# HGRN's first scaled level reads its keys from the forget gate, and the unit's output is written into the gate's own tile

## The chip, the cores and the metric

The kernel runs on one core of a Trainium2 chip. The metric is the device time of one launch in microseconds (us), smaller is better. Engine names are those of the profile: PE is TensorE's matmuls, PEld its weight loads, DVE is VectorE, ACT is ScalarE, POOL is GpSimd, SP is SyncE, which here only issues DMAs.

## The reference

The layer takes x (2048 rows of 1024, float32) through a mixer and a feed-forward part. The mixer has two groups of heads side by side; HGRN2 is the one that the change touches.

```python
def _hgrn2_mixer(q_raw, f_raw, i_raw, g_raw, lb, norm_w):
    f = lb + (1.0 - lb) * jax.nn.sigmoid(f_raw.astype(f32))
    q = heads(jax.nn.silu(q_raw.astype(f32))) * (HG_HEAD_DIM ** -0.5)
    k = heads(1.0 - f)
    logf = heads(jnp.log(f))
    v = heads(i_raw.astype(f32))
    o = _hgrn2_chunk_scan(q, k, v, logf)
    o = o * lax.rsqrt(jnp.mean(o * o, axis=-1, keepdims=True) + NORM_EPS)
    o = o.reshape(B, T, HG_WIDTH) * norm_w.astype(f32) * jax.nn.silu(g_raw.astype(f32))
...
def reference(...):
    proj = h @ w_in[l]
    ...
    x = x + jnp.concatenate([o_hg, o_rw], axis=-1) @ w_out[l]
    x = x + _conv_ffn(_rmsnorm(x, norm2_w[l]), w_up[l], conv_w[l], conv_b[l], w_down[l])
```

The scan is `o_t = S_t^T q_t` with `S_t = diag(f_t) S_{t-1} + k_t v_t^T`, per head of 128 columns. The keys are one minus the forget gate. The other group is RWKV-7, whose state update also has a solve of small triangular systems.

## The kernel before

Time is cut into 4 blocks of 512 steps. In the first part of the program (to about 1320 us) three streams are recorded in turn, a piece of each at a time: the *dense* stream (input projections, tile names pj, hh, hl, wh, wl, and output projections of finished blocks), the *RWKV* stream (`rw_super`, eight pieces, each two pairs of heads of one block) and the *HGRN* stream (`hg_unit`, sixteen units, one head of one block each, numbered here 0 to 15). All matmuls of the projections are three fp32r products (lines 270 to 272). The second part of the program, the feed-forward, comes after.

A scheduler takes the recorded instructions and sets a fixed order on each engine; an engine then runs its own list in that order and waits by semaphores for the others. Buffers come from pools: a tag names a ring of buffers, and a new tile of that tag waits until the readers of the tile that held the buffer have ended, a DMA that reads it included.

An HGRN unit takes q, f, v and the output gate gg from the projections (tags hq, hf, hv, hgg, two buffers each). Line 947 makes the keys k on VectorE in the one buffer of tag hk. Then come seven levels of `scaled`: at each, line 965 makes the query half of a tile X (tag hX, three buffers) by VectorE, and the key half is made by line 971, or at level 0 by a ScalarE copy; the running product Pf, which is f's own tile, and the running factor Sf are updated by lines 974 and 972. All ScalarE activations pass through the helper at line 122, so their line says 122 and the tile names tell them apart. The levels' matmuls are line 990 (and 997, 1046), masked into A and copied to Af. The state runs through lines 1044 to 1059, the output product through 1064 and 1065. The norm is the tail of the unit: squares into a tile osq that takes over the hk buffer, split into two parts, lines 1083 and 1084 sum them, and lines 1076 and 1077 multiply by the norm and the gate. Line 1078 stores the result to the DRAM tile oT, on SP's queue or, in the last block, on POOL's. Line 370 writes the gate tile when the projection's sum is evicted.

In the RWKV stream the names that matter are, in the order of the work: TZ and TTs, the inverted triangular blocks (lines 808, 814, and matmuls 821 and 834), L847, which applies them, the ScalarE copies of its results to UV and M, L867, the first matmul that needs the PSUM buffer which those copies free, and L881, whose results L884 and L887 (M and AR) take up on VectorE. L905 is the step of its state recurrence. Line 313 is the token shift of a projection's result rkv, and lines 241 to 243 are sums of tiles for the feed-forward, loaded from h2d.

Of the kernel before, what the change touches and what calls it, by code (L numbers as in the profile page):

```python
# [11 lines left out]
AF = mybir.ActivationFunctionType  # L12
# [6 lines left out]
P = 128  # L19
# [48 lines left out]
def tile_layer(ctx, tc, consts, x, norm1_w, w_in, hg_lb_logits, hg_norm_w, rw_shift_mu, rw_w0, rw_w2,  # L68
# [4 lines left out]
    V, S, TE = nc.vector, nc.scalar, nc.tensor  # L73
# [40 lines left out]
    def act(out_, in_, func, **kw):  # L114

        want = tables.get(func)
        if want is not None and want != tab["now"]:
            pre = S.preload_act_table_set(want)
            for u_ in tab["uses"]:
                tc.add_manual_dep(pre.ins, u_.ins.name, NOSYNC, reason="table order")  # L120
            tab.update(now=want, pre=pre, uses=[])
        i_ = S.activation(out_, in_, func, **kw)  # L122
        if want is not None:
            tc.add_manual_dep(i_.ins, tab["pre"].ins.name, NOSYNC, reason="table order")
            tab["uses"].append(i_)
        return i_
# [57 lines left out]
    oT = [dp.tile([D, BLK], F32, name=f"oT{b}") for b in range(NBLK)]  # L184
# [89 lines left out]
    def phase1(c1):  # L274
# [353 lines left out]
        def last_dma(nb):  # L628

            return nc.gpsimd.dma_start if nb == NBLK - 1 else dma  # L630
# [313 lines left out]
        def hg_unit(nb, j):  # L944
            q, f, v, gg = (stage.pop((n_, nb, j)) for n_ in "qfvg")
            k = rp.tile([P, BLK], F32, tag="hk", name="hk")
# [13 lines left out]
            def scaled(l):  # L960

                m = 1 << l
                X = rp.tile([P, BLK], F32, tag="hX", name="hX", bufs=3)
                vw = lambda t_: t_.rearrange("p (n e m) -> p n e m", e=2, m=m)
                V.tensor_mul(vw(X)[:, :, 1, :], vw(q)[:, :, 1, :], vw(Pf)[:, :, 1, :])
                n_ = BLK // (2 * m)
                if l == 0:
                    act(vw(X)[:, :, 0, :], vw(k)[:, :, 0, :], AF.Copy)
                    act(vw(Sf)[:, :, 0, :], vw(Pf)[:, :, 1, :], AF.Copy)
                else:  # L970
                    V.tensor_mul(vw(X)[:, :, 0, :], vw(k)[:, :, 0, :], vw(Sf)[:, :, 0, :])
                    V.tensor_mul(vw(Sf)[:, :, 0, :], vw(Sf)[:, :, 0, :],
                                 vw(Pf)[:, :, 1, m - 1:m].broadcast_to([P, n_, m]))
                V.tensor_mul(vw(Pf)[:, :, 1, :], vw(Pf)[:, :, 1, :],
                             vw(Pf)[:, :, 0, m - 1:m].broadcast_to([P, n_, m]))
                return X
# [32 lines left out]
            for l in range(3):  # L1009
                Xs.append(scaled(l))  # L1010
                yield
# [9 lines left out]
            for l in range(3, 6):  # L1021
                Xs.append(scaled(l))
                yield
# [9 lines left out]
            for c0 in range(0, P, 32):  # L1033
                act(Af[c0:c0 + 32, :, c0:c0 + 32], A[c0:c0 + 32], AF.Copy)
            yield
            X = scaled(6)
            V.tensor_mul(k, k, Sf)
            V.tensor_mul(q, q, Pf)
# [27 lines left out]
            sq = rp.tile([P, BLK], F32, tag="hk", name="osq")  # L1066
# [7 lines left out]
            act(sq, sq, AF.Exp, scale=-0.5)  # L1074
            yield
            V.tensor_mul(sq, op, sq)
            V.tensor_mul(sq, sq, gg)
            last_dma(nb)(oT[nb][j * P:(j + 1) * P, :], sq)
            done["hg"] += 1
            yield  # L1080

# [10 lines left out]
        def hg_stream():  # L1092
            for n in range(4 * NBLK):
                while ready["hg"] <= n:
                    yield None
                yield from hg_unit(n // 4, n % 4)
# [528 lines left out]
```

## Time and profile before

| | |
|---|---|
| median of 3 runs | 2646.72 us (2646.23 to 2655.82) |
| the profiled execution | 2645.42 us, span 2643.6 us |
| granted TensorE clock, mean | 0.994 |
| PE busy | 2547.0 us, 96% of the span |
| DVE busy | 1963.7 us, 74% |
| ACT busy | 1372.7 us, 52% |
| POOL busy | 382.1 us, 14% |
| HBM traffic | 192 GB/s over the span |
| chain that ended last | PE 70%, DVE 11%, ACT 8%, DMA 7%, issue 3% |

The profile is one execution. A row of a group gives line, engine, operation, output and inputs, shapes and count, then the busy time and the mean time of one, then the idle time of the engine before them and what ended it. A row of the timeline gives start and duration in us. In a row of waits the waiting instruction stands on the left of the arrow and the one that released it on the right.

### The profile page before, as it was taken

To read this page: it belongs to the slowest core of one execution; us is meant where nothing else is said; L and a number is where in the kernel's file an instruction comes from. 1 tells how busy PE (TensorE), PEld (TensorE's weight loads), DVE (VectorE), ACT (ScalarE), POOL (GpSimd) and SP (SyncE) were. 2 spreads that over 40 slices of the span, in tenths; PEclk is the share of its full clock that TensorE was granted. 3 is DMA by queue.
4 is the path that set the end of the run, shared out by engine and by line. 5 is a ranking of instruction groups with operands and counts; after the bars stand their busy time and mean duration, and the time that the engine had idled before them with its cause. 6 is when DMAs were issued, how large, how long until landed. Compare 5 with 4: busy or idle time off the path is not lost.

```text
span 2643.6 us, 51054 instructions
## 1 busy us (share of the span) xinstructions
PE 2547.0 (96%) x19467; PEld 2046.8 (77%) x19467; DVE 1963.7 (74%) x3744; ACT 1372.7 (52%) x2258; POOL 382.1 (14%) x686
## 2 busy tenths in 40 slices
PE   7999999999999999899899999999999999999998
PEld 5877777777777767777678888887888887888887
DVE  4868677676576765777678789988988887766556
ACT  5555444555545555344466654556554544545444
POOL 6433222212222122232100000000000000000000
PEclk9999999999999999999999999999999999999999
DMA  8846463555655565845583467747763553998655
GB/s 304 239 147 195 152 168 116 143 159 205 190 173 138 174 212 179 261 151 150 181 287 124 136 221 257 240 154 232 245 203 129 171 171 128 334 321 283 200 191 187
DMA packets 380298, 518.98 MB, mean 196 GB/s; under 512 B 114463, under 2 KB 211093, under 8 KB 380053
## 3 DMA queue, kind: packets, MB, share of 16 engines
q1 hardware_dynamic: 325521, 337.38, 40.1%
q0 software_dynamic: 54464, 178.32, 20.9%
q8 instruction: 153, 2.51, 0.4%
q14 instruction: 92, 0.75, 0.1%
q10 hardware_dynamic: 68, 0.02, 0.0%
HBM read 372.99 MB, written 134.22 MB: 192 GB/s over the span
## 4 chain that ended last, share of the span: by engine, by line
PE 70%; DVE 11%; ACT 8%; DMA 7%; issue 3%; POOL 0%; SPq 0%; DVEq 0%; ACTq 0%; POOLq 0%
PE pj L270 7%; PE pj L271 7%; PE pj L272 6%; PE ua L270 5%; PE ua L272 5%; PE ua L271 5%; PE da L271 3%; PE da L272 3%; PE da L270 3%; PE ud L271 2%; PE ud L270 2%; PE ud L272 2%; PE db L272 2%; PE db L271 2%; PE db L270 2%
## 5 line engine op out<-in xcount | busy, mean ns | idle before, releaser
L270 PE MATMUL pj<-hh,wh 128*128 128x512 f32 x960 | 391.6, 408 | 6.1 <-ACT rkv L122 4.0
L271 PE MATMUL pj<-hl,wh 128*128 128x512 f32 x960 | 377.4, 393 | 0.0
L272 PE MATMUL pj<-hh,wl 128*128 128x512 f32 x960 | 377.4, 393 | 0.0
L270 PE MATMUL ua<-Bh,uwh 128*128 128x512 f32 x704 | 276.4, 393 | 3.5 <-ACT m L122 2.2
L272 PE MATMUL ua<-Bh,uwl 128*128 128x512 f32 x704 | 274.3, 390 | 0.0
L271 PE MATMUL ua<-Bl,uwh 128*128 128x512 f32 x704 | 274.1, 389 | 0.0
L270 PEld LDWEIGHTS pj<-hh,wh 128*128 128x128 f32 x960 | 180.9, 189 | 54.5 <-issue 7.0
L272 PEld LDWEIGHTS pj<-hh,wl 128*128 128x128 f32 x960 | 180.8, 188 | 39.4 <-DMA wl<-Win171l 0.3
L271 PEld LDWEIGHTS pj<-hl,wh 128*128 128x128 f32 x960 | 181.0, 189 | 35.0 <-DVE hl L488 0.5
L254 ACT CAST uwh<-uraw 128x512 fp32r<-128x512 f32 x220 | 134.3, 617 | 135.0 <-PE ua L271 55.7
L255 DVE TENSOR_TENSOR dal<-draw,dah 128x512 fp32r<-128x512 f32 x138 | 95.2, 690 | 108.3 <-ACT dah L254 105.7
L255 DVE TENSOR_TENSOR uwl<-uraw,uwh 128x512 fp32r<-128x512 f32 x220 | 147.1, 684 | 34.3 <-ACT uwh L254 34.3
L254 ACT CAST dah<-draw 128x512 fp32r<-128x512 f32 x138 | 85.8, 621 | 160.0 <-PE da L271 75.5
L270 PEld LDWEIGHTS ua<-Bh,uwh 128*128 128x128 f32 x704 | 132.2, 188 | 33.9 <-ACT m L122 5.6
L272 PEld LDWEIGHTS ua<-Bh,uwl 128*128 128x128 f32 x704 | 132.2, 188 | 28.1 <-DVE uwl L255 0.4
L271 PEld LDWEIGHTS ua<-Bl,uwh 128*128 128x128 f32 x704 | 132.3, 188 | 26.7
L270 PE MATMUL ud<-Bh,uwh 128*128 128x512 f32 x352 | 138.0, 392 | 0.0
L1495 POOL DMA_DIRECT2D gd<-y x2 | 1.1, 542 | 943.1 <-DVE y L1493 943.1
L272 PE MATMUL ud<-Bh,uwl 128*128 128x512 f32 x352 | 137.1, 390 | 0.0
L271 PE MATMUL ud<-Bl,uwh 128*128 128x512 f32 x352 | 137.0, 389 | 0.0
L271 PE MATMUL da<-dbl,dah 128*128 128x512 f32 x332 | 129.4, 390 | 0.2 <-DVE dbl L255 0.2
L272 PE MATMUL da<-dbh,dal 128*128 128x512 f32 x332 | 129.2, 389 | 0.0
(582 smaller groups left out, 6203.0 us busy)
## 6 DMA issues: line engine op xcount, KB each, us to landing
uraw<-in_w_up_dram SPq DMA_DIRECT2D x176, 256.0 KB, 3.2
woraw<-in_w_out_dram POOLq DMA_DIRECT2D x96, 256.0 KB, 3.6
br<-gd SPq DMA_DIRECT2D x88, 256.0 KB, 4.3
draw<-Sg SPq DMA_DIRECT2D x88, 256.0 KB, 3.0
draw<-Tw SPq DMA_DIRECT2D x88, 256.0 KB, 3.9
gd<-y SPq DMA_DIRECT2D x86, 256.0 KB, 3.0
Sg<-br SPq DMA_DIRECT2D x72, 256.0 KB, 2.2
xt<-x1d SPq DMA_DIRECT2D x32, 512.0 KB, 6.5
```

The lines of the kernel that those rows point to most:

```text
L254: S.copy(hi, src)
L255: V.tensor_sub(lo, src, hi.bitcast(F32))
L270: TE.matmul(acc, lh, rh, start=first, stop=False, skip_group_check=skip)
L271: TE.matmul(acc, lh, rl, start=False, stop=False, skip_group_check=skip)
L272: TE.matmul(acc, ll, rh, start=False, stop=last, skip_group_check=skip)
L1495: (dma if end is None else nc.gpsimd.dma_start)(gd_[2 * h + b][fb * P:(fb + 1) * P, :], ys[0][:, b * BLK:(b + 1) * BLK])
```

## The change

At level 0 the key half of X is now computed by ScalarE from the even columns of f as −1·f + 1, where it was a copy of k's even columns. The tile k itself is still made on VectorE, for the diagonal matmuls, the later levels and the state. And the last product of the unit is written into the gate's tile gg, from which the store then reads; the squares' tile in the hk buffer is then free once VectorE has read it.

```diff
                 if l == 0:
-                    act(vw(X)[:, :, 0, :], vw(k)[:, :, 0, :], AF.Copy)
+                    act(vw(X)[:, :, 0, :], vw(f)[:, :, 0, :], AF.Identity, bias=1.0, scale=-1.0)
                     act(vw(Sf)[:, :, 0, :], vw(Pf)[:, :, 1, :], AF.Copy)
...
             V.tensor_mul(sq, op, sq)
-            V.tensor_mul(sq, sq, gg)
-            last_dma(nb)(oT[nb][j * P:(j + 1) * P, :], sq)
+            V.tensor_mul(gg, sq, gg)
+            last_dma(nb)(oT[nb][j * P:(j + 1) * P, :], gg)
```

The number of instructions per engine stays; the scheduler's order moves. Three places matter below. On ScalarE, at the start of unit 1, the copy stood between the token shift's rkv with a weight cast and the copies of UV and M:

```order
 L122 ACTIVATE rkv_1763<-pj,omu 128x512
 L254 CAST wh<-wraw 128x512
-L122 ACTIVATE hX<-hk 128x256
 L122 ACTIVATE UV<-rw 64x4x128 x4
 L122 ACTIVATE M<-rw 128x8x64
```

It is gone from there. Unit 1's copy now stands some thirty instructions earlier on ScalarE, between the eviction of its v (hv) and a cast, ahead of unit 0's copies to Af. The other odd units changed alike.

On VectorE, at the start of unit 13, just behind the last product of unit 12:

```order
-L1077 TENSOR_TENSOR osq<-osq,hgg 128x512
-L241 TENSOR_TENSOR xt<-xt 128x1024
-L242 TENSOR_TENSOR xt<-xt 128x1024
+L1077 TENSOR_TENSOR hgg<-osq,hgg 128x512
 L947 TENSOR_SCALAR hk<-hf 128x512
-L313 SCALAR_TENSOR_TENSOR rkv_13175<-pj,vt,rkv_13175 128x511
-L314 SCALAR_TENSOR_TENSOR rkv_13175<-lastc,vt,rkv_13175 128x1
 L974 TENSOR_TENSOR hf<-hf 128x256
-L315 COPY lastc<-pj 128x1
 L971 TENSOR_TENSOR hX<-hk,Sf 128x128x2
 L965 TENSOR_TENSOR hX<-hq,hf 128x128x2
 L972 TENSOR_TENSOR Sf<-Sf,hf 128x128x2
```

The keys and the first level's products moved ahead of the two sums of tiles (L241, L242) and of the token shift. Those come behind, then three products of the next level among them, and then L884 and L887.

On TensorE, between units 10 and 11, in the RWKV solve:

```order
+L834 MATMUL rw<-TTs,ZT 32x32
 L1083 MATMUL hg<-part,ones 128x512
-L270 MATMUL pj<-wh,hh 128x512
-L271 MATMUL pj<-wl,hh 128x512
-L270 MATMUL pj<-wh,hh 128x512
-L271 MATMUL pj<-wl,hh 128x512
+L834 MATMUL rw<-TTs,ZT 32x32 x31
+L1084 MATMUL hg<-part,ones 128x512
+L847 MATMUL rw<-RHS,TTs 64x128 x2
 L272 MATMUL pj<-wh,hl 128x512 x2
```

The solve's L821, L834 and L847 now come earlier among the projection matmuls, with the sums of unit 10's norm (L1083, L1084) in their midst, and L847 follows L834 directly where ten projection matmuls stood between them.

## The prediction

> **What bounds the kernel now.** I read the page's sums first, then busy time by stretch, then who waited for whom, then the timeline around the named waits.
>
> ```profile
> PE 2547.0 (96%) x19467; PEld 2046.8 (77%) x19467; DVE 1963.7 (74%) x3744; ACT 1372.7 (52%) x2258; POOL 382.1 (14%) x686
> ...
> core 0: us, PE busy (x) PEld busy (x) DVE busy (x) ACT busy (x) POOL busy (x), PEclk, DMA share, GB/s
> 60.00:1320.00 1260.00, 1194.66 (x13501) 935.24 (x13499) 882.50 (x2088) 637.02 (x1063) 329.47 (x592) 0.99 0.58 176
> 1320.00:2643.60 1323.60, 1307.92 (x5776) 1076.10 (x5776) 1052.51 (x1590) 705.14 (x1138) 14.04 (x26) 1.00 0.64 211
> ```
>
> TensorE is busy 96% of the span at a granted clock of 0.99 or 1.00. The change lies in the stretch from 60 to 1320 us, where the sixteen HGRN units run between the projections. There TensorE is idle 1260 − 1194.7 = 65.3 us. The change removes no matmul, so its gain is cut out of these 65.3 us (2.5% of the span). The question is which of that idle time ends on the two edited lines.
>
> ```profile
> PE rw L867 <- ACT M L122: 9.7, 6, 3.6
> PE rw L881 <- DVE AR L887: 4.3, 1, 4.3
> ...
> ACT hX L122 <- DVE hk L947: 20.1, 10, 5.8
> DVE M L884 <- PE rw L881: 16.8, 10, 5.3
> ...
>   DMA oT<-osq: 3.0, 2
> ```
>
> The columns are total us, times, longest. The second longest wait of TensorE is an RWKV matmul, L867, that waits for ScalarE's copy of M; it is no HGRN instruction. ScalarE in turn stands 20.1 us in ten waits for the HGRN keys, L947. The last row is VectorE's idle time before L947: twice it waited for the output store of the unit before. The timeline of unit 1 joins them (start, duration, engine, instruction; the idle time before it and its releaser in brackets):
>
> ```profile
> 143.68 0.69 DVE L1077 TENSOR_TENSOR osq<-osq,hgg 128x512 f32<-128x512 f32 x1
> 144.23 2.32 PE L847 MATMUL rw<-RHS,TTs 64*64 64x128 f32 x62
> 145.15 0.61 ACT L254 CAST wh<-wraw 128x512 fp32r<-128x512 f32 x1
> 148.94 0.43 DVE L947 TENSOR_SCALAR hk<-hf 128x512 f32<-128x512 f32 x1 [2.11 <-DMA oT<-osq]
> 149.40 0.45 ACT L122 ACTIVATE hX<-hk 128x256 f32<-128x256 f32 x1 [3.65 <-DVE hk L947]
> 149.86 2.40 ACT L122 ACTIVATE UV<-rw 64x512 f32<-64x512 f32 x4
> 152.27 1.82 ACT L122 ACTIVATE M<-rw 128x512 f32<-128x512 f32 x3
> 152.92 2.35 PE L867 MATMUL rw<-UV,KBT 128*64 128x64 f32 x37 [3.56 <-ACT M L122]
> ```
>
> Unit 0's output sits in the keys' buffer until its store has landed; then L947 writes the keys, ScalarE copies them, and only behind that copy, in ScalarE's order, come UV and M. So TensorE pays 3.56 us for a key copy of 0.45 us.
>
> **The change part by part.** *The copy from the gate.* It no longer reads k, and leaves its place ahead of UV (the ScalarE rows above). UV can then start when its matmul L847 has ended or ScalarE is free, whichever is later. In unit 1 that is 144.23 + 2.32 = 146.55 instead of 149.86: 3.31 us earlier, all of it inside the stall of 3.56, so 3.31 gained. Three other odd units show the same pattern:
>
> ```profile
> 292.85 2.13 PE L847 MATMUL rw<-RHS,TTs 64*64 64x128 f32 x62
> 296.39 2.41 ACT L122 ACTIVATE UV<-rw 64x512 f32<-64x512 f32 x4
> 299.46 1.26 PE L867 MATMUL rw<-UV,KBT 128*64 128x64 f32 x27 [1.53 <-ACT M L122]
> ...
> 428.52 2.24 PE L847 MATMUL rw<-RHS,TTs 64*64 64x128 f32 x64
> 431.06 2.42 ACT L122 ACTIVATE UV<-rw 64x512 f32<-64x512 f32 x4
> 434.13 2.06 PE L867 MATMUL rw<-UV,KBT 128*64 128x64 f32 x51 [0.43 <-ACT M L122]
> ...
> 907.51 0.62 ACT L254 CAST wh<-woraw 128x512 fp32r<-128x512 f32 x1
> 909.68 2.41 ACT L122 ACTIVATE UV<-rw 64x512 f32<-64x512 f32 x4
> 912.75 2.37 PE L867 MATMUL rw<-UV,KBT 128*64 128x64 f32 x64 [2.22 <-ACT M L122]
> ```
>
> Unit 3: 296.39 − 294.98 = 1.41, inside 1.53. Unit 5: 431.06 − 430.76 = 0.30, inside 0.43. Unit 11: the cast ends at 908.13, so 909.68 − 908.13 = 1.55, inside 2.22. In units 7, 9, 13 and 15 the copy is not what UV waits behind, and I count nothing.
>
> *The keys freed from the store.* L947 now follows L1077 directly. In unit 13 this also helps TensorE, since VectorE's order was rearranged there:
>
> ```profile
> 1108.78 1.23 DVE L241 TENSOR_TENSOR xt<-xt 128x1024 f32<-128x1024 f32 x1 [2.25 <-DMA xt<-h2d]
> ...
> 1111.19 0.42 DVE L947 TENSOR_SCALAR hk<-hf 128x512 f32<-128x512 f32 x1
> 1111.52 0.74 DVE L313 SCALAR_TENSOR_TENSOR rkv<-pj,vt,rkv 128x511 f32<-128x511 f32 x1
> ...
> 1113.71 0.69 DVE L884 TENSOR_TENSOR M<-rw,cst 128x512 f32<-128x512 f32 x1
> ...
> 1115.14 1.13 PE L881 MATMUL rw<-M 64*64 64x64 f32 x32 [4.31 <-DVE AR L887]
> ```
>
> L947 and the first four 256-column operations now run ahead of L241, in the 2.25 us in which VectorE waits for data; three operations of the next level come in between L241 and L884. From start to start one takes 1111.52 − 1111.19 = 0.33, so L884 moves up by 2 × 0.33 = 0.66 us and the stall of 4.31 shrinks by as much.
>
> *What the new form costs.* The matmul, VectorE and DMA counts stay. The copy gets a bias and a scale:
>
> ```profile
> L122 ACT ACTIVATE rkv<-pj,omu 128x512 f32<-128x512 f32 x43 | 29.4, 686 | 129.2 <-PE pj L272 129.2
> L122 ACT ACTIVATE hv<-pj 128x512 f32<-128x512 f32 x16 | 9.5, 596 | 45.0 <-PE pj L272 45.0
> L122 ACT ACTIVATE hX<-hk 128x256 f32<-128x256 f32 x16 | 7.1, 444 | 20.1 <-DVE hk L947 20.1
> ...
> 119.49 0.62 ACT L254 CAST wh<-wraw 128x512 fp32r<-128x512 f32 x1 [2.73 <-PE pj L271]
> ```
>
> An operand from a tile costs 686 − 596 = 90 ns, so the copy takes 0.44 (constant at no price) to 0.53 us. I take 0.53, at most 16 × 0.09 = 1.4 us of an engine that is half idle. Its new place in unit 1 is ahead of this cast, which idles 2.73 us waiting for TensorE; that idle time hides it. If the cover were gone in every unit, the casts and so TensorE would be late by 16 × 0.53 = 8.5 us. The new wait is for the hX buffer's last matmuls; in five of the eight odd units Af stands right behind it and waits for matmuls of that same group anyway, in unit 3 the copy waits for nothing, in units 1 and 11 a cast is behind it.
>
> *The store from the gate's tile.* L370 must now wait until the store of the output two units back has landed. The closest pair is:
>
> ```profile
> 1165.51 0.55 POOL L1078 DMA_DIRECT2D oT<-osq  x1 [1.22 <-DVE lastc L315]
> ...
> 1223.02 0.75 DVE L370 SCALAR_TENSOR_TENSOR hgg<-pj,vt,sgm 128x512 f32<-128x512 f32 x1
> ```
>
> 57 us lie between them. I cost it at nothing. If it did bite, the projections' evictions queue behind L370 and TensorE waits for banks.
>
> **The sum**: 3.31 + 1.41 + 0.30 + 1.55 + 0.66 = 7.2 us. What is late next is TensorE itself: VectorE's L884 waits for it 16.8 us in the rows above, so time won at L867 is handed on. The ceiling is these stalls whole: 9.7 + 4.3 = 14.0 us. The floor comes from the reordering at units 11, 13 and 15 (last rival). The profiled execution took 2645.42 us with a span of 2643.6, 1.3 us below the median 2646.72. From its own time the sum gives 2638.2, from the median 2639.5, which I forecast; its own range, with 3 us either way for waits that shift, is 2636 to 2643.
>
> **Rivals.**
> *The gain is swallowed.* The freed time reappears at later waits, because projections, weights and RWKV recurrence still arrive as before: within 2 us of 2646.7. For it: TensorE's 65 us of idle time is spread over many small waits. Against it: almost all end on ScalarE or VectorE work that TensorE's own progress releases. Chance 0.17. [...]
>
> *The stalls vanish whole.* M and AR are never late again and unit 11's earlier triangular solve adds nothing new: 2646.7 − 14.0 = 2632.7. For it: L821 moves ahead of the HGRN norm in unit 11. Against it: L847 sets when UV may start. Chance 0.10.
>
> *The new order costs more than the waits.* At unit 11 L847 now stands directly behind L834, where ten projection matmuls had covered ScalarE's copies of TTs; at units 13 and 15 the order was also redrawn. TensorE runs in order, so a late operand there holds all projection work behind it. Priced by the largest such stall in the rows, 4.31 us, at each of the three places: 12.9, less the 3.31 + 1.41 + 0.30 of the units left alone, is 7.9 slower: 2654.6. It decides once these new stalls exceed 5.0 us. Against it: TTs takes four copies of a few tenths of a us each. Chance 0.13.
>
> *The change does not do what it says*, that is, the copy still waits for L947 through another tile: then nothing moves; the redrawn order already shows the copy ahead of Af, so I leave it inside the first rival.
>
> **How the numbers follow.** Forecast 0.60, swallowed 0.17, whole 0.10, slower 0.13. A range from 2633 to 2650 holds the forecast, the swallowed gain and half of the whole gain around its 2632.7, and leaves out the slower case. What this kernel's measurement can tell from no change is about 0.5%, 13.2 us: below 2633.5 or above 2660. The first needs the whole gain or a little more (0.09), the second more than the slower rival's price (0.05); 0.86 remains for no difference.
>
> **What would show it.** In the profile after, the row of L867 waiting for ACT M should fall from 9.7 to about 3 us, ScalarE's 20.1 us wait for L947 and the two waits for the store should be gone, and TensorE's idle time from 60 to 1320 us should be near 58 us with its busy time unchanged. A stall at unit 11's L847 over 2 us, or L881 over 4.3 us in unit 13, would speak for the slower rival; an unchanged idle sum without the L867 row, for the swallowed gain. A wait of L370 for a DMA would show the store's tile mispriced.

## The result, and the profile after

The change runs in 2641.65 us (median of 13 runs, 2637.84 to 2643.87), the kernel before, on the same chip, in 2652.23 us (13 runs, 2645.53 to 2658.83). The ratio is 0.9966 with a 95% interval of 0.9956 to 0.9975: 9.0 us of 2652, between 6.6 and 11.7, and inside the 0.5% that the forecast called no difference. The forecast was 7.2 us less than before, 2639.5 us. It lies 2.2 us from the measured time, but on a base, 2646.72, that was the median of three runs and is 5.5 us below the median of 13; what is to be compared is the difference, 7.2 against 9.0. The profiled execution of the change took 2641.65 us, its span is 2639.9 us.

The mixer's stretch in the profile after, by the view that splits the span (busy time of each engine, granted clock, DMA share, GB/s):

```profile
60.00:1320.00 1260.00, 1202.79 (x13534) 940.44 (x13534) 887.67 (x2097) 640.32 (x1070) 328.90 (x592) 0.99 0.59 178
```

TensorE is idle for 1260 − 1202.8 = 57.2 us in it, where it was 65.3: 8.1 us less. Its busy time in this fixed stretch has grown by as much because work from behind 1320 us has moved in (13534 matmuls for 13501), so the "busy time unchanged" that the prediction named as a sign could not come with less idle time here. The table further down counts from matmul to matmul instead. The waits of the change:

```profile
DVE M L884 <- PE rw L881: 18.6, 10, 5.2
...
PE rw L881 <- DVE AR L887: 4.2, 1, 4.2
PE fa L271 <- DVE uwl L255: 4.1, 2, 3.1
PE rw L867 <- ACT M L122: 4.1, 7, 2.1
...
ACT hX L122 <- PE hg L990: 3.9, 4, 1.9
```

L867's wait for M fell from 9.7 to 4.1 us. Half of what is left, 2.06 us, is a stall in unit 9, where the copy never stood ahead of UV: it is 1.74, 2.05 and 2.06 us in three profiles of before. ScalarE's wait of 20.1 us for L947 has no row any more, nor has L947's for the store; L370 waits for no DMA. The copy has two new waits, 3.9 us in four for the last matmuls that read its ring buffer and 2.8 us in three for the gate itself (L354). AR's stall of 4.3 is 4.2. Rows of the timeline of unit 1 in the change:

```profile
118.12 0.44 ACT L122 ACTIVATE hX<-hf 128x256 f32<-128x256 f32 x1 [1.85 <-PE hg L990]
...
143.75 2.32 PE L847 MATMUL rw<-RHS,TTs 64*64 64x128 f32 x62
143.93 0.43 DVE L947 TENSOR_SCALAR hk<-hf 128x512 f32<-128x512 f32 x1
146.12 2.41 ACT L122 ACTIVATE UV<-rw 64x512 f32<-64x512 f32 x4 [0.84 <-PE rw L847]
148.54 1.81 ACT L122 ACTIVATE M<-rw 128x512 f32<-128x512 f32 x3
149.19 1.01 PE L867 MATMUL rw<-UV,KBT 128*64 128x64 f32 x15 [0.34 <-ACT M L122]
```

The copy runs at 118 us, long before UV; UV starts when L847 has ended (143.75 + 2.32 = 146.07), and L867 stands 0.34 us instead of 3.56.

### The profile page after: what moved, and what is told of

Read it like the earlier page. It is cut to its first block, busy times and chain, and to the rows that moved or that the text cites. A ratio compares the mean times of both kernels' runs of the same rounds, so it can differ in the third digit from the quotient of the medians.

```text
span 2639.9 us, 51054 instructions
## 1 busy us (share of the span) xinstructions
PE 2551.4 (97%) x19467; PEld 2046.3 (78%) x19467; DVE 1963.1 (74%) x3744; ACT 1371.3 (52%) x2258; POOL 381.4 (14%) x686
## 4 chain that ended last, share of the span: by engine, by line
PE 69%; DVE 13%; ACT 7%; DMA 7%; issue 4%; POOL 0%; SPq 0%; DVEq 0%; ACTq 0%; POOLq 0%
PE pj L270 7%; PE pj L271 7%; PE pj L272 7%; PE ua L270 4%; PE ua L272 4%; PE ua L271 4%; PE da L270 3%; PE da L271 3%; PE da L272 3%; PE ud L271 2%; PE ud L270 2%; PE ud L272 2%; PE db L272 2%; PE db L271 2%; PE db L270 2%
## 5 line engine op out<-in xcount | busy, mean ns | idle before, releaser
L270 PE MATMUL pj<-hh,wh 128*128 128x512 f32 x960 | 392.2, 409 | 4.5 <-ACT rkv L122 2.5
L271 PE MATMUL pj<-hl,wh 128*128 128x512 f32 x960 | 378.4, 394 | 0.0
L270 PE MATMUL ua<-Bh,uwh 128*128 128x512 f32 x704 | 276.8, 393 | 3.0 <-ACT m L122 2.5
L271 PE MATMUL ua<-Bl,uwh 128*128 128x512 f32 x704 | 274.2, 389 | 0.0
L270 PEld LDWEIGHTS pj<-hh,wh 128*128 128x128 f32 x960 | 181.2, 189 | 53.5 <-issue 8.3
L271 PEld LDWEIGHTS pj<-hl,wh 128*128 128x128 f32 x960 | 181.3, 189 | 35.3 <-issue 0.6
L255 DVE TENSOR_TENSOR dal<-draw,dah 128x512 fp32r<-128x512 f32 x138 | 95.2, 690 | 110.9 <-ACT dah L254 108.5
L255 DVE TENSOR_TENSOR uwl<-uraw,uwh 128x512 fp32r<-128x512 f32 x220 | 147.1, 684 | 32.8 <-ACT uwh L254 32.7
L270 PEld LDWEIGHTS ua<-Bh,uwh 128*128 128x128 f32 x704 | 132.3, 188 | 34.8 <-ACT m L122 7.0
L271 PEld LDWEIGHTS ua<-Bl,uwh 128*128 128x128 f32 x704 | 132.2, 188 | 26.6
L270 PE MATMUL ud<-Bh,uwh 128*128 128x512 f32 x352 | 138.0, 392 | 0.0
L271 PE MATMUL ud<-Bl,uwh 128*128 128x512 f32 x352 | 137.0, 389 | 0.0
L271 PE MATMUL da<-dbl,dah 128*128 128x512 f32 x332 | 129.5, 390 | 0.2 <-DVE dbl L255 0.2
```

The lines of the kernel that those rows point to most:

```text
L255: V.tensor_sub(lo, src, hi.bitcast(F32))
L270: TE.matmul(acc, lh, rh, start=first, stop=False, skip_group_check=skip)
L271: TE.matmul(acc, lh, rl, start=False, stop=False, skip_group_check=skip)
```

## The experiments

The theory: in units 1, 3, 5 and 11 the key copy stood in ScalarE's order ahead of UV and M, so TensorE waited at L867 for whatever made the copy late or long. The rivals: that the two edits are worth a part each; that reading the gate matters and not the copy's place; that the first profile had merely caught late stores; and that a gain or loss at L867 is swallowed further on.

**The first edit alone.**

```diff
-                    act(vw(X)[:, :, 0, :], vw(k)[:, :, 0, :], AF.Copy)
+                    act(vw(X)[:, :, 0, :], vw(f)[:, :, 0, :], AF.Identity, bias=1.0, scale=-1.0)
```

> The first edit alone: level 0 reads the gate, the output still goes to the hk buffer and is stored from there. Theory A (the two edits overlap: each takes the same stall of L867 away): UV is free of the copy, the row of L867 waiting for ACT M falls from 9.7 us to about 4, and the time falls by 7 to 9 us, ratio 0.9966 to 0.9975, although L947 still waits for the store (VectorE idle about 3 us before it). Rival B (the parts add up, since VectorE's wait for the store delays its own later work): about half the gain, 4 us, ratio near 0.9985.

Ratio 0.9977 (0.9965 to 0.9988). Its waits:

```profile
ACT hX L122 <- PE hg L990: 3.9, 4, 1.9
...
PE rw L867 <- ACT M L122: 3.5, 6, 1.9
```

**The second edit alone.**

```diff
-            V.tensor_mul(sq, sq, gg)
-            last_dma(nb)(oT[nb][j * P:(j + 1) * P, :], sq)
+            V.tensor_mul(gg, sq, gg)
+            last_dma(nb)(oT[nb][j * P:(j + 1) * P, :], gg)
```

> The second edit alone: the output goes to the gate's tile, level 0 still copies k and still stands ahead of UV on ScalarE. Theory A: k is made directly behind L1077, so the copy has run before L847 has ended and UV is not late; L867 waits about 4 us, the time falls by 7 to 10 us, ratio 0.9962 to 0.9973. TensorE's order at unit 11 stays that of before, with L847 in one piece, so it may be 1 to 2 us better than the change. Rival B (the parts add up): about 4 us, ratio near 0.9985.

Ratio 0.9973 (0.9960 to 0.9986). Its waits:

```profile
ACT hX L122 <- DVE hk L947: 7.9, 5, 3.3
...
PE rw L867 <- ACT M L122: 4.6, 7, 2.1
```

**Neither edit: the squares' tile in the ring of the X tiles**, so that the keys' buffer is free of the store, while the copy still reads the keys.

```diff
-            sq = rp.tile([P, BLK], F32, tag="hk", name="osq")
+            sq = rp.tile([P, BLK], F32, tag="hX", name="osq", bufs=3)
```

> Neither edit: level 0 copies k, the output is stored from the squares' tile, but that tile is taken from the ring of three hX buffers instead of the single hk buffer, so that nothing in the next unit's start waits for the store. Theory A (the store's landing is what held the copy): a gain like the change's, 7 to 10 us, ratio 0.9962 to 0.9973. Rival C (it is reading the gate or writing its tile that matters): no gain, 0.9990 to 1.0010. Both leave room for 2 us from the order, which moves in more places here.

Ratio 0.9979 (0.9965 to 0.9992). Its waits:

```profile
ACT hX L122 <- DVE hk L947: 5.6, 3, 3.3
...
DVE hX L965 <- DMA oT<-osq: 3.9, 1, 3.9
...
PE rw L867 <- ACT M L122: 3.8, 6, 2.1
```

**The change again**, beside these three.

> The change itself once more, beside the three others on the same chip: ratio 0.9966, between 0.9956 and 0.9975. Its second profile tells whether the 4.5 us that the first one lost after 1700 us, in the feed-forward, belong to the change (then they are there again) or to that execution (then not).

Ratio 0.9972 (0.9959 to 0.9984), L867's wait 3.2 us in six.

What follows from the four: each edit by itself takes L867 to 3.5 or 4.6 us, and both together to no less than about 3 to 4. In this wait they overlap; they don't add. The times alone don't decide it: the intervals of both single edits take in 0.9985, the half gain that the rival of added parts expected. Reading the gate is not what counts, since the ring variant has neither edit and the same row at 3.8. All four intervals overlap, so none of these versions is shown to be better than the change.

**The kernel before, profiled twice more.**

> The kernel before, unchanged, profiled again, to learn how much of a difference between two profiles is the execution's own. Theory (the gain is the L867 stall that ends on the key copy): the row of L867 waiting for ACT M stands again near 9.7 us, the wait of L947 for the store near 3.0 us in two, TensorE busy in 60 to 1320 near 1195 us. Rival (the first profile happened to catch the store late): the row of L867 falls towards the 3 to 4 us that the change showed, and the store wait with it. The feed-forward's stall near 1810 us, 1.55 in the first profile and 2.2 to 3.1 in the others, is free of both edits: if it also lies between 1.5 and 3 here, it is no effect of the change.

> As the run before it, a third profile of the kernel before: the same numbers expected, L867 for ACT M near 9.7 us by the theory and 3 to 4 by the rival; the feed-forward's stall near 1810 us anywhere from 1.5 to 3.

They took 2644.1 and 2646.9 us. The waits of the first of them:

```profile
PE rw L867 <- ACT M L122: 9.1, 7, 2.2
...
DVE hk L947 <- DMA oT<-osq: 2.7, 3, 1.3
```

And of the second:

```profile
PE rw L867 <- ACT M L122: 8.9, 6, 2.2
...
PE fa L271 <- DVE uwl L255: 4.2, 3, 3.0
```

L867's row is the kernel's own, 8.9 to 9.7 in three profiles. But its largest member is not: unit 1's stall was 3.56 us in the profile that I predicted from and 2.16 and 2.03 in these, where L947 waited 0.7 and 0.6 us for the store and not 2.1. In unit 13 it is the other way round: there L947 did not wait for the store in the first profile, and waited 1.28 and 1.02 us in these. The feed-forward's stall, L271 behind L255 near 1820 us, is 1.5, 2.0 and 3.0 us in the three profiles of before and 3.1 and 2.7 in the two of the change. It varies from execution to execution and is not shown to be an effect of the change.

**The stores issued by GpSimd, in the kernel before and in the change.** Line 1078 in both, shown for before:

```diff
-            last_dma(nb)(oT[nb][j * P:(j + 1) * P, :], sq)
+            store(oT[nb][j * P:(j + 1) * P, :], sq)
```

> The kernel before with the HGRN units' output stores issued on GpSimd's queue instead of SyncE's, so that the store's landing, for which L947 waits, comes later. Theory (the late store delays the keys, the copy, UV and so L867): the wait of L947 for the store grows from 3.0 us in two to about 7 us or more in three or more, L867 waiting for ACT M from 9.7 to 13 to 16 us, and the kernel is 4 to 8 us slower than before. Rival (the store isn't what delays the chain; the delay is in the order of the engines' work): the store's wait grows, but L867's row stays within 1 us of before's and the time within 2 us.

> The change with the same stores on GpSimd's queue. Theory: nothing waits for the store for 57 us, so its later landing costs nothing: no wait of L370 or L947 for a DMA, L867 for ACT M at 3 to 5 us, and the ratio to before is the change's, 0.996 to 0.998. Rival (moving stores onto GpSimd's queue costs by itself, by work behind them there): it is slower than the change by as much as the same move costs in the kernel before.

In the kernel before: ratio 0.9992 (0.9981 to 1.0003), the time of before, and not the 4 to 8 us more that I expected of it. The dose failed: L947 waited 2.2 us in four for the store, no longer than before, and L867's row is 7.8 us. But the scheduler redrew ScalarE's order, and unit 1 of this kernel's timeline became a cleaner experiment than the one meant:

```profile
146.52 2.41 ACT L122 ACTIVATE UV<-rw 64x512 f32<-64x512 f32 x4 [0.84 <-PE rw L847]
147.22 0.43 DVE L947 TENSOR_SCALAR hk<-hf 128x512 f32<-128x512 f32 x1 [0.47 <-DMA oT<-osq]
148.94 1.82 ACT L122 ACTIVATE M<-rw 128x512 f32<-128x512 f32 x3
149.59 2.47 PE L867 MATMUL rw<-UV,KBT 128*64 128x64 f32 x64 [0.32 <-ACT M L122]
...
151.28 0.44 ACT L122 ACTIVATE hX<-hk 128x256 f32<-128x256 f32 x1
```

The keys still wait for the store and the copy still reads them, but the copy stands behind UV and M, and the stall is 0.32 us, near the change's 0.34. It is the copy's place in the order that TensorE pays for. The change with stores on GpSimd: ratio 0.9975 (0.9961 to 0.9989), L867 3.3 us, no wait for a DMA: as the theory expected, although with the dose failed this says only that the move costs nothing there.

**The copy four times over, in the kernel before and in the change.** Line 968 in both, shown for before; the repeats write the same values.

```diff
-                    act(vw(X)[:, :, 0, :], vw(k)[:, :, 0, :], AF.Copy)
+                    for _ in range(4): act(vw(X)[:, :, 0, :], vw(k)[:, :, 0, :], AF.Copy)
```

> The kernel before with each level-0 key copy on ScalarE issued four times instead of once (three repeats that write the same values): 3 x 0.45 = 1.35 us more of ScalarE's time per unit, at the place of the copy. Theory (in the kernel before the copy stands ahead of UV and M in units 1, 3, 5 and 11, so that whatever lengthens it lengthens TensorE's stall at L867): the row of L867 waiting for ACT M grows from the 8.9 to 9.7 us of three profiles by about 4 x 1.35 = 5.4, to 13 to 15.5 us, and the kernel is 4 to 7 us slower than before, ratio 1.0015 to 1.0027. Rival (TensorE's later waits swallow what is lost at L867, as they would have swallowed a gain): L867's row grows, but the time stays within 2 us of before.

> The change with its copy from the gate issued four times, the same 3 x 0.5 us more of ScalarE's time per unit at the copy's new place, ahead of casts that wait for TensorE anyway. Theory (the new place is covered): L867's row stays at 3 to 5 us, and the time within 2 us of the change's, ratio to before 0.996 to 0.998. Rival (the cover is thin; the casts and evictions behind the copy become late): each unit pays up to 1.5 us, 10 to 24 us in all, ratio 1.001 to 1.006.

In the kernel before: ratio 1.0029 (1.0017 to 1.0041), 7.7 us slower. L867's row is 12.6 us, a little less than expected, and units 3, 5 and 11 of the timeline tell why:

```profile
295.07 1.88 ACT L122 ACTIVATE hX<-hk 128x256 f32<-128x256 f32 x4 [2.06 <-DVE hk L947]
296.97 2.40 ACT L122 ACTIVATE UV<-rw 64x512 f32<-64x512 f32 x4
300.03 3.96 PE L867 MATMUL rw<-UV,KBT 128*64 128x64 f32 x64 [2.76 <-ACT M L122]
...
435.19 1.89 ACT L122 ACTIVATE hX<-hk 128x256 f32<-128x256 f32 x4 [0.64 <-DVE hk L947]
437.09 2.41 ACT L122 ACTIVATE UV<-rw 64x512 f32<-64x512 f32 x4
440.16 2.47 PE L867 MATMUL rw<-UV,KBT 128*64 128x64 f32 x64 [1.76 <-ACT M L122]
...
918.55 0.45 ACT L122 ACTIVATE hX<-hk 128x256 f32<-128x256 f32 x1 [1.10 <-DVE hk L947]
919.02 2.40 ACT L122 ACTIVATE UV<-rw 64x512 f32<-64x512 f32 x4
922.09 2.37 PE L867 MATMUL rw<-UV,KBT 128*64 128x64 f32 x64 [2.22 <-ACT M L122]
```

Where all four copies stand ahead of UV, the stall grew from 1.39 to 2.76 and from 0.41 to 1.76 us (against the first of the two further profiles of before): 1.37 and 1.35 us, against some 1.4 us for the three added copies (1.88 − 0.45). In unit 11, and in unit 1, the scheduler put only one copy ahead, and unit 11's stall is 2.22, as before. Unit 1's is 3.29 us, but there L947 waited 1.79 us for the store, as in the first profile (2.11 us, stall 3.56). In units 3, 5 and 11 the stall follows the dose where the dose stands ahead of UV, and only there. In the change, the same repeats cost nothing that can be measured: ratio 0.9969 (0.9957 to 0.9981), L867 3.9 us. So its new place is covered, and the rival that every unit pays is out.

The swallowing rival expected the slower copies to leave the time within 2 us; it moved by 7.7, more than the row's growth of 12.6 − 9.2 (the mean of 9.7, 9.1 and 8.9) = 3.4, of which the dose makes 2.7. What may lie between is in the last section.

## Why the prediction was right, and where it wasn't

To compare executions piece by piece I count TensorE's projection and feed-forward products of lines 270, 1159 and 1270, which every version issues 3192 times, and take the time from one such product to a later one. From number 40 to 1240 covers the mixer; the shorter pieces hold the units named.

| from product to product (us) | before, three profiles | the change, two profiles | predicted | seen |
|---|---|---|---|---|
| 120 to 160, unit 1 | 57.9, 54.9, 54.9 | 53.1, 53.3 | −3.31 | −1.6 to −4.8 |
| 240 to 280, unit 3 | 54.9, 54.8, 54.8 | 53.1, 53.1 | −1.41 | −1.7 to −1.8 |
| 360 to 440, unit 5 | 106.0, 105.6, 105.9 | 106.1, 105.5 | −0.30 | about 0 |
| 760 to 840, unit 11 | 99.8, 99.8, 100.4 | 101.4, 104.8 | −1.55 | +1.0 to +5.0 |
| 960 to 1000, unit 13 | 63.2, 62.7, 62.7 | 59.2, 61.9 | −0.66 | −0.8 to −4.0 |
| 1080 to 1120, unit 15 | 63.6, 64.8, 63.1 | 62.7, 62.4 | 0 | −0.4 to −2.4 |
| 40 to 1240, the mixer | 1283.7, 1284.4, 1281.1 | 1275.2, 1278.8 | −7.2 | −2.3 to −9.2 |
| its TensorE idle time | 66.2, 62.0, 64.9 | 57.2, 58.6 | −7.2 | −3.4 to −9.0 |

- *The bound, and the link from the key copy to L867*: right, and shown by the repeated copies and by the order that the GpSimd stores brought about. L867's row was to fall to about 3 us and stood at 4.1 and 3.2.
- *Unit 1, 3.31 us*: right for the profile it was read from, too much for the kernel. Stalls of 2.16 and 2.03 us in the two further profiles, with 0.3 left in the change, make it some 1.8, and so does the piece (54.9 to 53.1 or 53.3). The 57.9 us of the first profile hold the longer stall and 1.7 us of halved clock behind it (last section). One execution's store wait was taken for the rule.
- *Unit 3, 1.41 us*: right; the piece is 1.7 us shorter. *Unit 5*: the stall fell from 0.43 to 0.18 as reckoned, but the piece is no shorter.
- *Unit 11, 1.55 us*: wrong in sign, although its stall did fall from 2.22 to 0.39. What failed is the step "the cast ends, so UV starts 1.55 us earlier, all gained": it priced the stall and not the redrawn order beside it. L847's 64 matmuls, one block of 1.98 us before, are scattered among the projections in the change:

```profile
894.95 0.43 PE L847 MATMUL rw<-RHS,TTs 64*64 64x128 f32 x4
896.45 0.65 PE L847 MATMUL rw<-RHS,TTs 64*64 64x128 f32 x8
898.15 0.88 PE L847 MATMUL rw<-RHS,TTs 64*64 64x128 f32 x22
900.59 0.44 PE L847 MATMUL rw<-RHS,TTs 64*64 64x128 f32 x4
901.62 1.08 PE L847 MATMUL rw<-RHS,TTs 64*64 64x128 f32 x26
```

  By these rows they occupy 3.5 us in five pieces, 1.5 us more; since a row overlaps the next a little, from each start to the next start it is 3.2 us against 1.9, 1.3 us more. The slower rival named this place, but as a stall of 4.31 us behind late operands; there was none, and the price was TensorE's own busy time. In the whole piece that is 94.3 to 94.6 us in three profiles of before and 97.0 in the first of the change, at a full clock in all four, while the idle time fell from between 5.4 and 5.8 us to 4.4: some 2.6 us lost, half of it on L847, and some 1.2 won. The first edit alone, the change with stores by GpSimd and the change with four copies, which scatter L847 too, have 97.0 or 97.1; the second edit alone, which leaves it whole, has 94.7. The second profile of the change is longer again, 104.8 us, because its clock was at half for 6.8 us from 895.7 us on, which takes 3.4 us. What stays open is the second edit alone: with L847 whole and a stall of 1.21 its piece is no faster than before either (100.9 us).
- *Unit 13, 0.66 us*: right on VectorE: L884 starts 4.13 and 4.14 us behind L241 in the change and 4.93 in the profile that I used, 0.80 less. In the further profiles of before it is 6.30 and 6.04, because L947 stands between them and waits for the store:

```profile
1108.44 0.43 DVE L947 TENSOR_SCALAR hk<-hf 128x512 f32<-128x512 f32 x1 [1.28 <-DMA oT<-osq]
```

  AR's stall was to shrink by 0.66 from 4.31; it was 5.5 and 6.3 in the further profiles of before, and 4.2 and 3.4 in the change. The profile that I used had caught it at its shortest of the three. How much of the piece's gain is this term stays open: the first edit alone keeps VectorE's old order here (4.93 us) and has a stall of 4.1 and a piece of 60.8 us, the second edit alone has the new order, a stall of 4.8 and 62.0 us.
- *Unit 15*, costed at nothing by either term, is shorter as well; why is not shown.
- *The copy's price, 0.53 us, hidden*: it takes 0.44 us, as the plain copy did (means of 440 and 444 ns), so the constant scale and bias cost nothing that shows, and the cover is real, as the repeats show. *The store from the gate's tile, at nothing*: right.

That the sum came out near the measured gain is in part luck: unit 1's term was 1.5 us too large, unit 11's 1.55 had the wrong sign, and units 13 and 15 won more than the 0.66 that was counted for them. The idle time of TensorE in the mixer fell by 6.5 us on the means, 64.4 to 57.9, beside the forecast 7.2; the mixer by 6.1, 1283.1 to 1277.0; the timed ratios say 9.0 (6.6 to 11.7) and, in the second comparison, 7.4 (4.2 to 10.9) us.

## What to carry to other kernels

Before removing a late operand, look where its consumer stands in its engine's order: a cheap instruction costs what is queued behind it, and any one edit that moves it or frees its input may bring the whole gain, so two such edits need not add. Read a stall from several executions before it becomes a term of a sum, and when an edit redraws the order, price the new order too, not only the stall that goes. A dose test (the suspected instruction several times over, in its old place and in its new) tells position from size within one comparison.

## What the runs showed of the hardware

**Some stalls are paid twice.** With about half of TensorE's longer stalls its granted clock falls to half for 3.4 us or more. In the five profiles of before and the change there are 34 stalls of 1.95 us and more between 60 and 1320 us; with 18 of them, among these all six of 3.3 us and more, the clock is at half at some time between their start and 3.5 us past their end. In the kernel before, behind unit 1's stall of 3.56 us, by windows of 2 us:

```profile
152.00:154.00 2.00, 0.98 (x18) 0.88 (x20) 0.72 (x2) 1.95 (x4) 0.00 (x0) 0.90 0.00 0
154.00:156.00 2.00, 2.00 (x43) 2.00 (x42) 0.00 (x0) 1.19 (x3) 0.49 (x1) 0.50 0.03 8
156.00:158.00 2.00, 2.00 (x79) 1.81 (x76) 0.00 (x0) 0.00 (x0) 0.05 (x1) 0.74 0.35 131
```

The clock is the third number from the end. Two us times the shortfalls 0.10 + 0.50 + 0.26 is 1.7 us lost, or 3.4 us at half clock. In the kernel with four copies the longer stall of unit 3 had the same effect, for 6.8 us (299.29 to 306.12 in the trace's clock records), of which three windows:

```profile
300.00:302.00 2.00, 1.97 (x33) 1.97 (x35) 0.00 (x0) 1.18 (x2) 0.00 (x0) 0.50 0.03 8
302.00:304.00 2.00, 2.00 (x41) 1.88 (x40) 0.00 (x0) 0.00 (x0) 0.00 (x0) 0.50 0.00 0
304.00:306.00 2.00, 2.00 (x65) 1.88 (x65) 0.03 (x1) 0.00 (x0) 0.00 (x0) 0.50 0.00 0
```

L867's 64 matmuls took 3.96 us there against 2.37 at full clock, and the piece of unit 3 grew by 4.1 us (54.8 to 58.9) for a stall 1.37 us longer. Adding up 2 us times one minus the granted clock over the windows below 0.98 from 60 to 1320 us gives 13.6, 20.5 and 13.6 us for the three profiles of before, 10.2 and 11.9 for the change and 23.9 for before with four copies. My sum had no such term. It may be what the repeats lost beyond L867's row: from product 40 to 1240 TensorE's busy time is 1225.9 us there, for the same matmuls, against 1217.5, 1222.4 and 1216.2 before. But that is one profile, and the 20.5 us show how far the sum moves without any edit; the mixer of that execution was hardly longer, 1284.4 us. The change's busy time over the same products, 1218.0 and 1220.2 us, is not below before's, so what it won is idle time; a gain in clock, if there was one, is not seen beside what unit 11's new order cost.

A stall of 2 or 3 us does not always draw it: in before, L270 stalls for 3.10 us up to 991.16 us at a full clock. L443 stalls for 1.98 us in unit 2, by the timeline of before:

```profile
218.82 0.66 PE L443 MATMUL pj<-ident,xt 128*128 128x128 f32 x4 [1.98 <-ACT hf L122]
```

and by that of the change:

```profile
213.54 0.66 PE L443 MATMUL pj<-ident,xt 128*128 128x128 f32 x4 [1.98 <-ACT hf L122]
```

In before, the clock stays at 1.00 behind it:

```profile
218.00:220.00 2.00, 0.90 (x5) 0.61 (x5) 2.00 (x4) 1.99 (x4) 0.47 (x1) 1.00 0.00 0
220.00:222.00 2.00, 1.65 (x11) 1.04 (x10) 2.00 (x3) 2.00 (x5) 1.33 (x3) 1.00 0.55 158
```

In the change it is halved:

```profile
214.00:216.00 2.00, 1.72 (x8) 1.22 (x7) 2.00 (x3) 1.91 (x4) 1.29 (x2) 0.72 0.34 129
216.00:218.00 2.00, 2.00 (x9) 1.67 (x8) 2.00 (x3) 1.62 (x4) 0.97 (x2) 0.50 0.66 205
```

In the Trainium skill's "TensorE: Matmul & The Clock Gate", the section "Part 1: The HAM clock gate (the "warmup" mystery)" describes a window of activity of about 3.4 us that runs freely. The traces agree: in the clock records of all these runs the stretches at half clock between 60 and 1320 us last 3.41, 6.83 or 10.24 us, and in each execution their starts lie whole multiples of 3.413 us apart (in before 153.62 and 498.36 us, 101 of them). Where a stall falls on that grid should then matter, and the two rows of L443 fit: in before a window ends at 218.47 us, within the stall, and the windows on its two sides have 1.63 and 0.98 us of TensorE idle time; in the change the whole stall lies in one window, 211.46 to 214.87 us, with 2.26 us idle, and the next window is at half clock. No threshold comes out of this: 1.31 us idle in the window up to 416.26 us of the change sufficed, 1.83 us in the one up to 989.88 us of before did not. The same page's rule in "HAM oscillation — how this bites in real kernels", no TensorE gaps above about 3.4 us, is too generous here, where 1.98 us sufficed.

**Small matmuls lost by being scattered.** The five pieces of L847 above took 1.3 us more than the one block, from start to next start, in busy time that no wait explains. It is 3.2 us in the four profiles with scattered pieces at a full clock, and 1.9 in the six that keep the block.
